# A new order of the mixing stage's stream, and new rules for when background steps are put in, in a two-layer fp32 decoder trunk

## The chip, the core and the metric

One core of a Trainium2 chip runs the whole program. The metric is device time in microseconds of one execution; the time of a kernel is the median of its runs. TensorE (PE) does the matmuls, VectorE (DVE) and ScalarE (ACT) the elementwise work, GpSimd (POOL) a few adds and small transfers, SyncE (SP) issues the weight loads. Each engine works through its own instructions in the order in which they were written, and waits where an input isn't there.

## What is computed

Two layers, each a half-step SwiGLU FFN, a mixing stage, and a second half-step FFN, over 256 tokens of width 1024, then a final RMS norm. The mixing stage is the part that changes:

```python
h = rms_norm(x, mix_norm[l])
(u, q_b, c_kv, q_i, k_i, w_i, q_c, k_c, v_c, f_c, g_a, g_b, g_c) = split(h @ w_in[l])
a = s5_branch(u, ...)                      # diagonal state space, then a GLU (w_glu)
b = dsa_branch(q_b, c_kv, q_i, k_i, w_i, ...)   # indexer picks 64 keys a query, then attention
c = fox_branch(q_c, k_c, v_c, f_c + fox_b_f[l]) # attention with a cumulative forget gate
merged = (sigmoid(g_a) * (a @ w_branch_ssm[l]) + sigmoid(g_b) * (b @ w_branch_dsa[l])
          + sigmoid(g_c) * (c @ w_branch_fox[l]))
x = x + merged @ w_out[l]
```

## The kernel before

**The stream.** Every weight matrix is cut into units of 2 x 128 rows and at most 512 columns (512 KB), in the order in which PE uses them (`plan`, whose mixing part follows the table `ORDER`). A unit is loaded by SP into one of four `raw` buffers, split by ACT into a rounded high part (`hi`) and by DVE into the rest (`lo<-raw,hi`), and multiplied on PE in three passes, hi x hi, lo x hi and hi x lo, for each of two halves of the tokens: 12 matmuls of 512 columns a unit. These matmuls write `ps_acc` and are called the stream here. The stream has nothing to wait for but its units, and its left side: `h0`, `h1` are the two halves of the normed input (h and l: high and low part), `ath`, `atl` the FFN's activations, `ahl` the state space's result, `bh`, `bl` the result of one of the two attentions.

**The background.** All else is written as Python generators that are stepped between the stream's matmuls while the program is built: `ssm` (state space; its matmuls read `u4` and `state`), `indexer` (scores and eight rounds of top-8 on DVE, then attention of DSA), `latent` (keys and values of DSA), `forget` (cumulative sums, sent through DRAM to the tiles `fm`), `fox` (attention of FoX), and the transposes of the next stage's input (`norm_T`, tiles `ps_t<-ident,...`). An attention (`attend`) goes in three pairs of heads. Each pair takes scores on PE (`kdT,qbT` or `kcT,qcT`), a sum with a bias and a minimum on DVE (`st,mn<-ps_t,bm` or `fm`; the biases come from POOL), four exponentials on ACT, a scaling by the sums' reciprocal, then for each head three transposes on PE (`ident,st`) and a copy to `pt`, and the product with the values (`pt,vd` or `pt,vs`), whose result is split into `bh` and `bl`. These matmuls write `ps_t`, in four banks that are used in turn.

**What sets the order.** `tick` is called after every three to six stream matmuls. It keeps a clock of its own for each engine, first splits ahead (`feed`: high parts up to 4 units ahead, low parts up to 3), and then steps the first background generator, by rank, whose input is ready by that clock and while neither DVE nor ACT is more than `BACKLOG` (1.25 us of that clock) ahead of PE. `rank` is 2 for the indexer and its attention, 1 for `latent` and `forget`, 3 for FoX, 4 for the state space, which counts as rank 0 from a set time on (`due`, in steps of `PACE`, 25 us). Where the stream comes to a branch whose attention isn't finished, `finish` steps that generator to its end with no stream in between.

**The table.** `ORDER` sets the mixing stage's second half. Before: both gates of DSA, both of FoX, one of the state space, branch DSA (first half of the output columns), branch FoX, gate SSM, GLU, then the other branches, SSM last. `merged` of a half is complete with its third branch; its transposes make the left side of `w_out`. The four gates of DSA and FoX and the first of the state space are 5 x 48 stream matmuls; all the rest of the second half, up to `w_out`, is 48 of gate, 24 short ones of the GLU and 96 of branches.

Of the kernel before, what the change touches and what calls it, by code (L numbers as in the profile page):

```python
# [41 lines left out]
SB, CH, NB = 4, 32, T // 4  # L42


ORDER = [("gate", "dsa", 0), ("gate", "dsa", 1), ("gate", "fox", 0), ("gate", "fox", 1), ("gate", "ssm", 0),
         ("branch", "dsa", 0), ("branch", "fox", 0), ("gate", "ssm", 1),
         ("glu", "ssm", 0), ("branch", "dsa", 1), ("branch", "ssm", 0), ("branch", "fox", 1), ("branch", "ssm", 1)]
GATE = {"ssm": 0, "dsa": 1, "fox": 2}
BRANCH_K = {"ssm": 2, "dsa": 3, "fox": 3}

# [5 lines left out]
HI_AHEAD, LO_AHEAD = 4, 3  # L56
# [4 lines left out]
LATENCY, SAME = 0.2, 0.13  # L61


TICK, BACKLOG, PREP, EAGER = 1.5, 1.25, 0.0, -0.5

FEED, PACE = 0.3, 25.0

LAST = 8

# [55 lines left out]
class Clock:  # L125
# [9 lines left out]
    def ready(self, ap, eng=None):  # L135
        t, by = self.done.get(ap.tensor.name, (0.0, eng))
        return t + (SAME if by == eng else LATENCY)
# [16 lines left out]
    def late(self, eng, cost, out, src):  # L154
        self.t[eng] += 1.0
        self.done[out.tensor.name] = max(self.t[eng], self.ready(src)) + cost + 3.0, "dma"
# [76 lines left out]
class Trunk:  # L233
    def __init__(self, ctx, tc, a, out):
        self.clock = Clock()
        self.tc, self.nc, self.a, self.out = tc, Engines(tc.nc, self.clock), a, out
        self.ctx = ctx
        nc = self.nc
        pool = lambda **kw: ctx.enter_context(tc.tile_pool(**kw))

        self.const = pool(name="const", bufs=1, side="right")
        self.rawp = pool(name="raw", bufs=RAW_BUFS, side="right")
        self.small = pool(name="small", bufs=2, side="right")
        self.hpool = pool(name="h", bufs=1, side="left")
        self.piecep = pool(name="piece", bufs=1, side="left")
        self.accp = pool(name="acc", bufs=4, space=PSUM)
        self.tp = pool(name="tps", bufs=T_BANKS, space=PSUM)
        self.dram = pool(name="scratch", bufs=2, space=DRAM)
        self.tlive, self.tcount = {}, 0
        self.bg, self.wait, self.rank, self.due, self.backlog = [], {}, {}, {}, {}  # L250

        self.units = plan(a)
        self.raw, self.split_tiles, self.freed = {}, {}, {}
        self.n_dma = self.n_hi = self.n_lo = self.n_used = 0
# [26 lines left out]
    def spawn(self, gen, rank=0, backlog=BACKLOG):  # L281
        self.rank[gen] = rank
        self.wait[gen] = None
        self.due[gen], self.backlog[gen] = math.inf, backlog
        self.bg.append(gen)
        return gen

    def urgency(self, g):
        return self.rank[g] if self.clock.t["pe"] < self.due[g] else 0

    def step(self, g):
        self.now = g
# [12 lines left out]
        w = self.wait[g]  # L305
        return self.clock.ready(w) if isinstance(w, bass.AP) else 0.0

    def feed(self):

        now, ready = self.clock.t["pe"] + FEED, self.clock.ready  # L310
        while self.n_hi < min(self.n_used + HI_AHEAD, self.n_dma) and ready(self.raw[self.n_hi]) <= now:
            self.feed_hi(self.n_hi + 1)
        while self.n_lo < min(self.n_used + LO_AHEAD, self.n_hi) and ready(self.split_tiles[self.n_lo]) <= now:
            self.feed_lo(self.n_lo + 1)

    def tick(self):
        t = self.clock.t
        now = t["pe"]
        while t["pe"] < now + TICK:
            self.feed()  # L320
            for g in sorted(self.bg, key=self.urgency):
                if not self.blocked(g) and self.when(g) <= t["pe"] + EAGER and max(t["dve"], t["act"]) <= now + self.backlog[g]:
                    self.step(g)
                    break
            else:
                return

    def finish(self, *gens):
# [351 lines left out]
    def mix(self, l, nxt):  # L680
# [5 lines left out]
        with tc.tile_pool(name="mix", bufs=1, side="left") as pool:  # L686
# [35 lines left out]

            self.rows_read = self.qk_read = False
            gen_x = self.spawn(self.indexer(l, xs), 2)
            gen_s = self.spawn(self.ssm(l, uT), 4)


            vs = pool.tile([P, 2, VW], F32, name="vs")
# [16 lines left out]
            for k0 in (0, 4):  # L745
                self.mm_col(pk, self.hx, k0, 4, 256, 0, 7)
            self.scaled(kcT[:, 1:3], pk, rb, 2)
            gen_f = self.spawn(self.fox(gen_g, qcT, kcT, vs), 3)

            qbT = pool.tile([P, 3, T], F32, name="qbT")  # L750
            pq = self.acc()
# [63 lines left out]
    def indexer(self, l, xs):  # L815
        nc, pool = self.nc, self.mp
        stt = nc.vector.scalar_tensor_tensor

        kd = pool.tile([P, 2, 2, HD], F32, tag="kd", name="kd")
        nc.vector.tensor_copy(kd, xs[:, :, KI:KI + HD].unsqueeze(2).to_broadcast([P, 2, 2, HD]))  # L820
        wi = pool.tile([P, 2, 4], F32, name="wi")
        self.ts(wi, xs[:, :, WI:WI + 4], 0.5)
        yield xs
        i, ps = yield from self.bank()
        for h in range(2):
            for t in range(2):
                nc.tensor.transpose(ps[:, h * T + t * P:h * T + t * P + P], xs[:, t, QI + h * P:QI + h * P + P], self.ident)
        yield ps
        qk = pool.tile([P, 3, T], F32, tag="bh2", name="qk")
        qiT, kiT = qk[:, :2], qk[:, 2]  # L830
        nc.scalar.activation(qiT, ps.rearrange("p (k t) -> p k t", k=2), AF.Copy, scale=0.125)
        self.tfree(i)
        yield kd
        i, ps = yield from self.bank()
        for t in range(2):
            nc.tensor.transpose(ps[:, t * P:t * P + P], kd[:, t].rearrange("p a b -> p (a b)"), self.ident)
        yield ps
        nc.scalar.activation(kiT, ps[:, :T], AF.Copy)
        self.tfree(i)
        yield kiT  # L840

        score = pool.tile([P, 384], F32, tag="pt1", name="score", bufs=2)
        for p in range(2):
            got = yield from self.banks()
            for q, k in ((slice(P, T), slice(0, T)), (slice(0, P), slice(0, P))):
                for e, (i, ps) in enumerate(got):
                    r = slice(e * HD, e * HD + HD)
                    o = ps[:, P:384] if q.start else ps[:, 0:P]
                    nc.tensor.matmul(o, qiT[r, p, q], kiT[r, k], start=True, stop=True)
            yield got[1][1]  # L850
            rel = pool.tile([P, 2, 384], F32, tag="st1", name="rel", bufs=2)
            for e, (i, ps) in enumerate(got):
                h = 2 * p + e
                nc.scalar.activation(rel[:, e], ps[:, :384], AF.Relu)
                self.tfree(i)
                for c, t, n in self.PARTS:
                    b = self.ccm[:, T - n:] if h == 0 else score[:, c]
                    stt(score[:, c], rel[:, e, c], wi[:, t, h:h + 1], b, op0=OP.mult, op1=OP.add)
                if e == 0:
                    yield  # L860
        self.qk_read = True

        sc = pool.tile([P, 2], F32, name="sc")
        for t in range(2):
            j = self.small.tile([P, 512], F32, tag="junk", name="junk", bufs=1)
            nc.scalar.activation(j[:, :P], xs[:, t, CKV:CKV + P], AF.Square, accum_out=sc[:, t:t + 1])
        latent = self.spawn(self.latent(l, xs, sc), 1)

        for rd in range(TOPK // 8):
            for c, t, n in self.PARTS:  # L870
                m8 = pool.tile([P, 8], F32, tag="m8", name="m8", bufs=2)
                nc.vector.max(m8, score[:, c])
                nc.vector.match_replace(score[:, c], m8, score[:, c], -3e38)
                yield
        madd = pool.tile([P, 384], F32, name="madd")
        self.ts(madd, score, -2e38, NEG, OP.is_gt, OP.mult)

        def bias(p):
            bm = pool.tile([P, 2, 384], F32, tag="bm", name="bm")
            for c, t, n in self.PARTS:  # L880
                nc.gpsimd.tensor_tensor(bm[:, :, c], madd[:, c].unsqueeze(1).to_broadcast([P, 2, n]),
                                        self.biasT[:, 2 * p:2 * p + 2, T - n:], op=OP.add)
            return bm

        yield latent
        yield lambda: self.rows_read
        yield from self.attend(self.qbT, lambda p, r: self.kdT[r, :], bias, lambda h, t: self.vd[:, t], "1")
# [162 lines left out]
    def ssm(self, l, uT):  # L1050
        nc, pool = self.nc, self.mp
        tt = nc.vector.tensor_tensor
        gen, begin = self.now, self.clock.t["pe"]
        quads = [(slice(m * CH, m * CH + CH), slice(i * CH, i * CH + CH), m, i) for m in range(4) for i in range(SB)]
        late = lambda n: self.due.__setitem__(gen, begin + n * PACE)
        late(0)
        yield uT

        u4 = pool.tile([P, 8, NB], F32, tag="u4", name="u4")
# [2 lines left out]
            if i == SB - 1:  # L1062
                yield

        late(1)
        w = pool.tile([P, 2, 8, NB], F32, tag="w", name="w")
        st = pool.tile([P, 2, 8, NB], F32, tag="st", name="state")
        half = [P, 2, 4, NB]
# [1 line left out]
        for h in (0, 4):  # L1070
# [31 lines left out]
            tt(st[:, 0, hs], g1[:, 0], g2[:, 1], op=OP.subtract)  # L1102
            tt(st[:, 1, hs], g1[:, 1], g2[:, 0], op=OP.add)
            yield
            late(2)

        late(3)
        yield st
        i, y = yield from self.bank()
        y = y.rearrange("p (c t) -> p c t", c=8)  # L1110
# [386 lines left out]
```

## Time and profile before

| | us |
|---|---|
| median of 3 runs (1246.01 to 1247.59) | 1246.51 |
| the profiled execution | 1247.36 |
| its span, first to last instruction | 1245.6 |
| PE busy in the span | 1189.1 (95%) |
| DVE busy | 789.2 (63%) |
| ACT busy | 605.2 (49%) |

The profile shows one execution. Its own time is 0.85 us above the median; sums over its rows are made against its own time. A matmul's end in the trace is modelled and overlaps the next one, so what a matmul costs is read from one start to the next. The two mixing stages lie at 210 to 437 us and at 822 to 1048 us.

### The profile page before, as it was taken

Reading aid. Unit: us, or ns where it says so; the run is one execution under the profiler, and the core shown is the slowest. Engines: PE = TensorE matmul, PEld = TensorE weight load, DVE = VectorE, ACT = ScalarE, POOL = GpSimd, SP = SyncE. Lnnn points to the kernel's source line nnn. Section 1 sums busy time; section 2 is a strip of 40 time slices with the busy share of each in tenths; the row PEclk is TensorE's granted clock in tenths of the full one; section 3 lists DMA queues with packets and bytes.
Section 4 is the critical chain, followed back from the end, with each engine's and each line's share of the span. In section 5 each row is a group of like instructions: output and inputs, shape, how many; then the busy total and the mean of one; then the engine's idle time right before and its main releaser. Section 6 shows DMA issues by size and latency. Waiting matters only on the chain. (4 is left out here: it accounts for less than half of the span.)

```text
span 1245.6 us, 16482 instructions
## 1 busy us (share of the span) xinstructions
PE 1189.1 (95%) x5990; PEld 992.7 (80%) x5990; DVE 789.2 (63%) x1382; ACT 605.2 (49%) x887; POOL 87.7 (7%) x135
## 2 busy tenths in 40 slices
PE   8999999999869899999999999999997789999997
PEld 6788888998648778888888888889885577888886
DVE  4886855787646665555577645567875575655554
ACT  5544444644544454444455445446546345544442
POOL 1000600000310510000000000000021000000000
PEclk9999999999879999999999999999999799999999
DMA  8665745575314566647565646555652155665552
GB/s 273 203 181 158 228 151 147 153 227 173 94 43 152 153 181 188 188 132 228 190 186 169 171 142 220 186 147 162 206 162 81 56 181 156 200 186 170 178 191 88
DMA packets 115554, 208.07 MB, mean 167 GB/s; under 512 B 7486, under 2 KB 27376, under 8 KB 115472
## 3 DMA queue, kind: packets, MB, share of 16 engines
q1 hardware_dynamic: 114000, 203.51, 53.8%
q0 software_dynamic: 1184, 3.11, 0.9%
q8 instruction: 47, 0.77, 0.3%
q10 hardware_dynamic: 288, 0.39, 0.1%
q14 instruction: 35, 0.29, 0.1%
HBM read 205.91 MB, written 1.07 MB: 166 GB/s over the span
## 5 line engine op out<-in xcount | busy, mean ns | idle before, releaser
L216 DVE TENSOR_TENSOR lo<-raw,hi 128x1024 fp32r<-128x1024 f32 (+3 forms) x415 | 472.1, 1143 | 291.1 <-PE ps_acc L216 208.6
L216 ACT ACTIVATE hi<-raw 128x1024 fp32r<-128x1024 f32 (+3 forms) x415 | 410.3, 991 | 459.5 <-PE ps_acc L216 397.9
L216 PE MATMUL ps_acc<-hi,h0h 128*128 128x512 f32 (+3 forms) x544 | 211.8, 389 | 7.2 <-ACT h0h L216 3.5
L216 PE MATMUL ps_acc<-hi,h0l 128*128 128x512 f32 (+3 forms) x544 | 206.1, 379 | 6.2 <-DVE h0l L216 6.2
L216 PE MATMUL ps_acc<-lo,h0h 128*128 128x512 f32 (+3 forms) x544 | 205.6, 378 | 2.0 <-DVE lo L216 2.0
L216 PE MATMUL ps_acc<-hi,h1h 128*128 128x512 f32 (+3 forms) x544 | 205.4, 377 | 0.0
L216 PE MATMUL ps_acc<-hi,h1l 128*128 128x512 f32 (+3 forms) x544 | 203.9, 375 | 0.0
L216 PE MATMUL ps_acc<-lo,h1h 128*128 128x512 f32 (+3 forms) x544 | 203.7, 375 | 0.0
L216 PE MATMUL ps_acc<-hi,ath 128*128 128x512 f32 x352 | 139.8, 397 | 0.0
L216 PE MATMUL ps_acc<-hi,atl 128*128 128x512 f32 x352 | 137.1, 390 | 0.0
L216 PE MATMUL ps_acc<-lo,ath 128*128 128x512 f32 x352 | 137.1, 389 | 0.0
L216 PEld LDWEIGHTS ps_acc<-hi,h0h 128*128 128x128 f32 x544 | 103.2, 190 | 26.9 <-ACT h0h L216 4.5
L216 PEld LDWEIGHTS ps_acc<-hi,h0l 128*128 128x128 f32 x544 | 103.0, 189 | 25.8 <-DVE h0l L216 7.5
L216 PEld LDWEIGHTS ps_acc<-lo,h0h 128*128 128x128 f32 x544 | 103.3, 190 | 19.7 <-DVE lo L216 3.5
L216 PEld LDWEIGHTS ps_acc<-hi,h1l 128*128 128x128 f32 x544 | 102.3, 188 | 17.9
L216 PEld LDWEIGHTS ps_acc<-hi,h1h 128*128 128x128 f32 x544 | 102.4, 188 | 17.8 <-issue 0.2
L216 PEld LDWEIGHTS ps_acc<-lo,h1h 128*128 128x128 f32 x544 | 102.5, 188 | 17.3
L216 PEld LDWEIGHTS ps_acc<-hi,ath 128*128 128x128 f32 x352 | 66.1, 188 | 14.1 <-issue 1.1
L216 PEld LDWEIGHTS ps_acc<-hi,atl 128*128 128x128 f32 x352 | 66.1, 188 | 14.1
L216 PEld LDWEIGHTS ps_acc<-lo,ath 128*128 128x128 f32 x352 | 66.1, 188 | 13.6 <-issue 0.5
L216 PE MATMUL ps_t<-ident,st 128*128 128x128 f32 x72 | 16.9, 371 | 29.6 <-ACT st L216 23.6
L216 DVE SCALAR_TENSOR_TENSOR act<-ps_acc,rstd,s 128x512 f32<-128x512 f32 (+1 forms) x48 | 32.0, 704 | 15.7 <-PE ps_acc L216 15.6
(270 smaller groups left out, 1266.7 us busy)
## 6 DMA issues: line engine op xcount, KB each, us to landing
raw<-in_ffn_w_down_dram SPq DMA_DIRECT2D x88, 512.0 KB, 4.2
raw<-in_ffn_w_up_dram SPq DMA_DIRECT2D x80, 512.0 KB, 3.8
raw<-in_ffn_w_gate_dram SPq DMA_DIRECT2D x79, 512.0 KB, 3.8
raw<-in_w_in_dram SPq DMA_DIRECT2D x56, 512.0 KB, 4.3
raw<-in_w_out_dram SPq DMA_DIRECT2D x16, 512.0 KB, 3.7
raw<-in_ffn_w_gate_dram SPq DMA_DIRECT2D x18, 256.0 KB, 2.8
raw<-in_ffn_w_up_dram SPq DMA_DIRECT2D x16, 256.0 KB, 2.8
raw<-in_w_in_dram SPq DMA_DIRECT2D x16, 256.0 KB, 2.8
```

The costliest lines, as they stand in the source:

```text
L216: return f(*args, **kw)
```

## The change

The table puts the state space first: its two gates, DSA's gates, the GLU, one gate of FoX, both branches of the state space, branch DSA, the last gate of FoX, and then the last three attention branches. The state space's rank becomes 3 and FoX's 4, `latent` goes from 1 to 2, and the due times are gone. In `tick`, low parts are first split only 2 units ahead and high parts 3; then background steps are taken, as long as DVE and ACT are within 8 us of PE (1.25 before) and the next low and high part still have room before the time at which PE will want them; only when no step is to be had are the parts split up to 3 and 4 ahead, as before. A step may be taken when its input is ready 0.2 us ahead of PE, 0.5 before. What is computed stays the same: PE has the same 5502 instructions in both programs.

```diff
-ORDER = [("gate", "dsa", 0), ("gate", "dsa", 1), ("gate", "fox", 0), ("gate", "fox", 1), ("gate", "ssm", 0),
-         ("branch", "dsa", 0), ("branch", "fox", 0), ("gate", "ssm", 1),
-         ("glu", "ssm", 0), ("branch", "dsa", 1), ("branch", "ssm", 0), ("branch", "fox", 1), ("branch", "ssm", 1)]
+ORDER = [("gate", "ssm", 0), ("gate", "ssm", 1), ("gate", "dsa", 0), ("gate", "dsa", 1), ("glu", "ssm", 0), ("gate", "fox", 0),
+         ("branch", "ssm", 0), ("branch", "ssm", 1), ("branch", "dsa", 0), ("gate", "fox", 1),
+         ("branch", "fox", 0), ("branch", "dsa", 1), ("branch", "fox", 1)]
...
-TICK, BACKLOG, PREP, EAGER = 1.5, 1.25, 0.0, -0.5
-
-FEED, PACE = 0.3, 25.0
+TICK, BACKLOG, PREP, EAGER = 1.5, 8.0, 0.0, -0.2
+
+
+FEED, FIRST, UNIT, LO_ROOM, HI_ROOM = 0.3, (3, 2), 2.7, 2.0, 3.5
...
+    def spare(self, i):
+
+        return self.clock.t["pe"] + sum(UNIT * m * n / 1024 for _, m, n in self.units[self.n_used:i])
+
+    def room(self, backlog, now):
+
+        dve, act = self.clock.t["dve"], self.clock.t["act"]
+        if max(dve, act) > now + backlog:
+            return False
+        return self.n_lo == len(self.units) or dve < self.spare(self.n_lo) - LO_ROOM and act < self.spare(self.n_hi) - HI_ROOM
...
         while t["pe"] < now + TICK:
-            self.feed()
-            for g in sorted(self.bg, key=self.urgency):
-                if not self.blocked(g) and self.when(g) <= t["pe"] + EAGER and max(t["dve"], t["act"]) <= now + self.backlog[g]:
+
+            self.feed(*FIRST)
+            for g in sorted(self.bg, key=self.rank.get):
+                if not self.blocked(g) and self.when(g) <= t["pe"] + EAGER and self.room(self.backlog[g], now):
                     self.step(g)
                     break
             else:
+                self.feed()
                 return
```

**First place: PE, DSA's attention in layer 0.** `ident,st` are the transposes of the weights of one head, `kdT,qbT` the scores of a pair, `pt,vd` and `pt,vs` the products with the values of DSA and FoX. Before, after the last matmul of the last gate:

```order
L216 MATMUL ps_acc<-hi,h1l 128x512
L216 MATMUL ps_t<-ident,st 128x128 x3
L216 MATMUL ps_t<-kdT,qbT 128x256 x2
L216 MATMUL ps_t<-kdT,qbT 128x128 x2
L216 MATMUL ps_t<-ident,st 128x128 x3
L216 MATMUL ps_t<-pt,vd 64x256 x2
L216 MATMUL ps_t<-pt,vd 64x128 x2
L216 MATMUL ps_t<-ident,st 128x128 x6
```

Now, at the last of DSA's first branch and the first of FoX's second gate:

```order
L217 MATMUL ps_acc<-lo,bh 128x512
L217 MATMUL ps_acc<-hi,bl 128x512
L217 MATMUL ps_t<-ident,st 128x128 x3
L217 MATMUL ps_acc<-hi,h0h 128x512
L217 MATMUL ps_acc<-lo,h0h 128x512
L217 MATMUL ps_acc<-hi,h0l 128x512
...
L217 MATMUL ps_t<-pt,vs 64x256 x2
L217 MATMUL ps_t<-pt,vs 64x128 x2
```

Before, steps of the attentions follow each other on PE; now stream matmuls stand between a head's transposes and the product that needs their copy, six of them here.

**Second place: PE, the end of the branches in layer 0.** `ident,gate` are the transposes of `merged`, `ahl` is the state space's branch, `h0h` after them the left side of `w_out`. Before:

```order
L216 MATMUL ps_acc<-lo,ahl 128x512
L216 MATMUL ps_acc<-hi,ahl 128x512
L216 MATMUL ps_t<-ident,gate 128x128 x8
L216 MATMUL ps_acc<-hi,h0h 128x512
L216 MATMUL ps_acc<-lo,h0h 128x512
L216 MATMUL ps_acc<-hi,h0l 128x512
L216 MATMUL ps_t<-ident,gate 128x128 x4
```

Now, in the last half unit of DSA's second branch, ahead of the 18 matmuls of FoX's second branch:

```order
L217 MATMUL ps_acc<-hi,bl 128x512
L217 MATMUL ps_t<-ident,gate 128x128 x4
L217 MATMUL ps_acc<-hi,bh 128x512
L217 MATMUL ps_acc<-lo,bh 128x512
L217 MATMUL ps_acc<-hi,bl 128x512
L217 MATMUL ps_t<-ident,gate 128x128 x4
```

Before, the first eight transposes stand right ahead of the matmul that needs their result; now the branch stands between.

**Third place: DVE, DSA's attention in layer 0.** `lo<-raw,hi` is the low part of a unit. Before:

```order
L216 ISA st,mn<-ps_t,bm 128x256
L216 ISA mn 128x1
L216 TENSOR_TENSOR lo<-raw,hi 128x1024 x2
L216 COPY vT<-v 32x128 x5
L216 TENSOR_TENSOR lo<-raw,hi 128x512
L216 COPY vT<-v 32x128 x3
L216 RECIPROCAL ri<-rs 128x4
```

Now:

```order
L217 ISA st,mn<-ps_t,bm 128x256
L217 ISA mn 128x1
L217 TENSOR_TENSOR lo<-raw,hi 128x1024
L217 COPY vT<-v 32x128 x8
L217 TENSOR_TENSOR bl<-ps_t,bh 128x256
L217 RECIPROCAL ri<-rs 128x4
L217 TENSOR_SCALAR st<-st,ri 128x256
L217 TENSOR_TENSOR lo<-raw,hi 128x1024
```

The low parts have moved behind steps of the attentions and of the state space.

## Rows read from the trace of the kernel before

**Rows 1.** Page, part 2: busy tenths in 40 slices of the span.
```profile
PE   8999999999869899999999999999997789999997
DVE  4886855787646665555577645567875575655554
```
**Rows 2.** Windows: stretch, length, busy (count) of PE, PEld, DVE, ACT, POOL; clock, DMA.
```profile
209.97:329.96 119.99, 119.99 (x732) 108.27 (x730) 94.73 (x221) 67.40 (x108) 11.06 (x13) 1.00 0.58 172
329.96:375.59 45.63, 30.62 (x143) 19.54 (x141) 21.17 (x76) 19.38 (x61) 7.76 (x7) 0.71 0.12 40
375.59:462.31 86.72, 81.86 (x375) 67.27 (x375) 58.59 (x83) 42.80 (x57) 21.84 (x44) 0.98 0.53 164
942.01:984.76 42.75, 27.63 (x143) 17.73 (x141) 21.23 (x76) 19.26 (x61) 7.61 (x7) 0.83 0.13 42
984.76:1073.16 88.40, 83.53 (x375) 68.59 (x375) 58.15 (x83) 42.79 (x57) 0.56 (x1) 0.95 0.53 167
```
**Rows 3.** Windows round single groups; a window's count includes a neighbour or two.
```profile
462.31:468.71 6.40, 6.40 (x33) 5.29 (x32) 4.63 (x7) 3.10 (x4) 0.00 (x0) 1.00 0.67 180
245.71:251.47 5.76, 5.76 (x51) 5.76 (x50) 5.26 (x25) 1.34 (x4) 0.00 (x0) 1.00 0.35 104
313.33:314.18 0.85, 0.85 (x10) 0.69 (x9) 0.12 (x1) 0.60 (x1) 0.85 (x1) 1.00 0.04 12
958.34:959.53 1.19, 1.19 (x9) 0.69 (x9) 0.89 (x5) 0.61 (x3) 0.00 (x0) 1.00 0.00 0
...
334.33:335.52 1.19, 0.00 (x0) 0.00 (x0) 1.19 (x9) 0.86 (x4) 0.00 (x0) 0.90 0.00 0
```
**Rows 4.** Chain of waits, a piece of the last FFN: start, us, what.
```profile
763.39 32.68 PE ps_acc L216 x144
```
**Rows 5.** Timeline of PE, layer 0's attentions; in brackets idle before, and releaser.
```profile
337.22 1.95 PE L216 MATMUL ps_t<-ident,st 128*128 128x128 f32 x6 [3.68 <-ACT st L216]
339.11 2.25 PE L216 MATMUL ps_t<-pt,vd 128*64 128x256 f32 x8
...
342.44 0.82 PE L216 MATMUL ps_t<-kcT,qcT 64*128 64x256 f32 x8
345.64 1.54 PE L216 MATMUL ps_t<-ident,st 128*128 128x128 f32 x6 [2.38 <-ACT st L216]
...
349.16 0.50 PE L216 MATMUL ps_acc<-hi,bh 128*128 128x512 f32 x1
...
371.93 1.54 PE L216 MATMUL ps_t<-ident,st 128*128 128x128 f32 x6 [3.10 <-ACT st L216]
...
375.59 0.79 PE L216 MATMUL ps_acc<-hi,bh 128*128 128x512 f32 x1
```
**Rows 6.** Timeline of PE and DVE, start of w_out and of layer 0's second FFN.
```profile
407.82 1.03 PE L216 MATMUL ps_t<-ident,gate 128*128 128x128 f32 x8
412.92 0.50 PE L216 MATMUL ps_acc<-hi,h0l 128*128 128x512 f32 x1 [3.09 <-DVE h0l L216]
...
412.18 1.28 DVE L216 SCALAR_TENSOR_TENSOR h0l<-ps_t,h0h 128x512 fp32r<-128x512 f32 x2
...
439.44 0.50 PE L216 MATMUL ps_acc<-hi,h0h 128*128 128x512 f32 x1 [1.52 <-ACT h0h L216]
```
**Rows 7.** Timeline of POOL: a pair of bias adds, beside low parts and alone.
```profile
319.51 2.94 POOL L216 TENSOR_TENSOR bm<-madd,biasT 128x256 f32<-128x256 f32 x2 [2.31 <-DVE mn L216]
...
335.67 1.97 POOL L216 TENSOR_TENSOR bm<-madd,biasT 128x256 f32<-128x256 f32 x2 [13.22 <-DVE mn L216]
```
**Rows 8.** Waits over the whole span: us in total, times, longest us.
```profile
DVE lo L216 <- PE ps_acc L216: 208.6, 145, 4.1
```
**Rows 9.** DMA issues: KB each, median us from issue to landing.
```profile
raw<-in_w_in_dram SPq DMA_DIRECT2D x56, 512.0 KB, 4.3
...
fm<-cumd POOLq DMA_DIRECT2D x6, 256.0 KB, 4.0
cumd<-cum POOLq DMA_DIRECT2D x2, 6.0 KB, 3.3
```

More of the change, by code (lines that the diff above doesn't have):

```diff
@@ L249, in __init__ @@
         self.tlive, self.tcount = {}, 0
-        self.bg, self.wait, self.rank, self.due, self.backlog = [], {}, {}, {}, {}
+        self.bg, self.wait, self.rank, self.backlog = [], {}, {}, {}
         self.units = plan(a)
@@ L283, in spawn @@
         self.wait[gen] = None
-        self.due[gen], self.backlog[gen] = math.inf, backlog
+        self.backlog[gen] = backlog
         self.bg.append(gen)
         return gen
-    def urgency(self, g):
-        return self.rank[g] if self.clock.t["pe"] < self.due[g] else 0
     def step(self, g):
@@ L306, in when, with feed @@
         return self.clock.ready(w) if isinstance(w, bass.AP) else 0.0
-    def feed(self):
+    def feed(self, hi=HI_AHEAD, lo=LO_AHEAD):
         now, ready = self.clock.t["pe"] + FEED, self.clock.ready
-        while self.n_hi < min(self.n_used + HI_AHEAD, self.n_dma) and ready(self.raw[self.n_hi]) <= now:
+        while self.n_hi < min(self.n_used + hi, self.n_dma) and ready(self.raw[self.n_hi]) <= now:
             self.feed_hi(self.n_hi + 1)
-        while self.n_lo < min(self.n_used + LO_AHEAD, self.n_hi) and ready(self.split_tiles[self.n_lo]) <= now:
+        while self.n_lo < min(self.n_used + lo, self.n_hi) and ready(self.split_tiles[self.n_lo]) <= now:
             self.feed_lo(self.n_lo + 1)
+    def spare(self, i):
[5 more added lines that the diff above has]
+        return self.n_lo == len(self.units) or dve < self.spare(self.n_lo) - LO_ROOM and act < self.spare(self.n_hi) - HI_ROOM
     def tick(self):
@@ L724, in mix @@
             gen_x = self.spawn(self.indexer(l, xs), 2)
-            gen_s = self.spawn(self.ssm(l, uT), 4)
+            gen_s = self.spawn(self.ssm(l, uT), 3)
             vs = pool.tile([P, 2, VW], F32, name="vs")
@@ L747, in mix @@
             self.scaled(kcT[:, 1:3], pk, rb, 2)
-            gen_f = self.spawn(self.fox(gen_g, qcT, kcT, vs), 3)
+            gen_f = self.spawn(self.fox(gen_g, qcT, kcT, vs), 4)
             qbT = pool.tile([P, 3, T], F32, name="qbT")
@@ L866, in indexer @@
             nc.scalar.activation(j[:, :P], xs[:, t, CKV:CKV + P], AF.Square, accum_out=sc[:, t:t + 1])
-        latent = self.spawn(self.latent(l, xs, sc), 1)
+        latent = self.spawn(self.latent(l, xs, sc), 2)
         for rd in range(TOPK // 8):
@@ L1052, in ssm @@
         tt = nc.vector.tensor_tensor
-        gen, begin = self.now, self.clock.t["pe"]
         quads = [(slice(m * CH, m * CH + CH), slice(i * CH, i * CH + CH), m, i) for m in range(4) for i in range(SB)]
-        late = lambda n: self.due.__setitem__(gen, begin + n * PACE)
-        late(0)
         yield uT
@@ L1063, in ssm @@
                 yield
-        late(1)
         w = pool.tile([P, 2, 8, NB], F32, tag="w", name="w")
@@ L1104, in ssm @@
             yield
-            late(2)
-        late(3)
         yield st
```

## Prediction

> **What bounds the kernel now.** I read the page's slices first: PE is busy nine tenths or more nearly everywhere, but falls to 8, 6, 9 and 7, 7, 8, 9 tenths near the ends of the two mixing stages, where DVE has no more to do than elsewhere [rows 1]. So PE bounds the time, and what a change of order can win is the time in which PE stands or runs slowly. The windows show where that is. Layer 0's mixing runs for its first 119.99 us with PE busy throughout, at full granted clock, though fourteen groups of background matmuls stand in that stretch and DVE is busy 94.73 us of it, 79% [rows 2]. Then come 45.63 us in which PE is busy 30.62, at a mean granted clock of 0.71, and 86.72 us with 81.86 busy; layer 1 repeats this with 42.75 and 88.40 us [rows 2]. The timeline shows what those 45.63 us are: the transposes wait 3.68, 2.38, 3.10 us for ACT's share of the softmax, with nothing else on PE [rows 5]. This is `finish`, called by the first attention branch with both attentions still open.
>
> What PE's work there would cost with nothing to wait for, by start-to-start times at full clock: 144 stream matmuls in 32.68 us, 0.227 each [rows 4]; 48 of 256 columns in 5.76, 0.12 each; 24 stream matmuls and 8 transposes in 6.40, so 0.95 for the 8, 0.12 each; a pair's scores 0.85; a pair's product with the values 1.19 [rows 3]. The 45.63 us hold 142 of these (a window counts a neighbour more): 36 transposes 4.3, five pairs of scores 4.25, six products 7.1 and 18 stream matmuls 4.1, in all 19.8. **Lost: 25.8 us in layer 0, and 22.9 of the same 19.8 in layer 1** (42.75). The next stretch holds 374: 318 stream matmuls 72.2, 24 short ones 2.9, 32 transposes 3.8, in all 78.9. **Lost: 7.8 and 9.5 us.** Its two visible places are the start of w_out, 3.09 us behind eight transposes put right ahead of their use, and the second FFN's first matmul, 1.52 us [rows 6]; most of the rest is the lower clock, 0.98 and 0.95. In sum 66.0 us of the two mixing stages are loss.
>
> **The change part by part.** *The table.* No instruction comes or goes on PE. The state space's gates take the place of FoX's as cover for the indexer, at no cost, since both have 48 matmuls of the same kind. What counts is that the attentions' steps now stand among stream matmuls: from the first scores of DSA to the last product of FoX 192 of them (43.6 us) and 24 short ones (2.9). In the order I count 23 background groups there in each layer, with 0.7 to 2.7 us of stream ahead of most.
>
> Is that enough for the chains? FoX's took 33.2 us in the open, from 342.44 to 375.59, with the clock at half for much of it [rows 5]. Between the same two steps PE now has 129 stream matmuls (29.3), 24 short ones (2.9), ten groups of three transposes (3.6), three of scores (2.6) and five products (6.0): 44.4 us. DSA's took 35.8, from 313.33 to 349.16 [rows 3, 5]; between its first scores and last product stand 135 stream matmuls (30.6), 24 short ones (2.9), eight groups of transposes (2.9), six of scores (5.1) and four products (4.8), 46.3 us, and the state space's output besides. So each chain has some 11 us to spare where it had none, and **25.8 and 22.9 us come back, less what single groups still wait.**
>
> *What single groups wait.* No row shows these steps in this cover, so I bound it. From below: 0, as in the first 119.99 us, with groups of the same length behind 0.7 to 5 us of stream [rows 2]. It can't be less, since a group costs its own time. From above: in the open a group waits 2.4 to 3.7 us [rows 5]; with some 2 us of stream ahead of each on average (46.5 over 23), the groups could wait about 1 us each, 23 us a layer. The row nearest is the covered stretch: DVE's load decides, and with 174.5 us of DVE work a layer over the 219 that remain (94.73 + 21.17 + 58.59, over 252.3 less the 33) it is 80%, against 79% there. I take 3 us a layer for the smaller margin (0.2 for 0.5 us), and keep 0 to 12 in the forecast.
>
> *The end of the branches.* The transposes of `merged`'s first half now stand 18 matmuls, 4.1 us, ahead of w_out. After them come two copies on ACT and two on DVE, which took 1.28 us at 412.18 [rows 6]. So the 3.09 us go in both layers, and nothing is late next: the second half has 21 matmuls of cover. The second FFN's first transposes stand 15 matmuls ahead of their use, where they stood 3 and 0, so the 1.52 us go too. Where PE was busy throughout the clock was 1.00 [rows 2], so the 7.8 and 9.5 us come back whole.
>
> *Background ahead of low parts.* In front of one low part, that of the unit used right after DSA's first product, DVE now has two pairs' sums, 1.19 us each [rows 3], a dozen short steps and the part itself: 5 to 6 us, an estimate from those rows. PE has 4.5 us of work from the unit before to that one (eleven stream matmuls, a pair's scores, a product). Cost on PE: nothing, if DVE is ahead by more than the difference. DVE waited 145 times for PE with a low part, 208.6 us in all [rows 8], so it is ahead as a rule; that cover gone, such a unit would cost about 1 us. SP's loads follow the low parts, which free the buffers; a unit lands in 4.3 us [rows 9], and four buffers hold 10.9 us of stream (48 matmuls), so they stay hidden.
>
> *POOL.* Its six pairs of adds a layer now all run beside low parts. FoX's first bias needs the sums' write (3.3 us), the read back (4.0) and a pair of adds of about 2: 9.3 us behind DVE's scan [rows 9, 7]; PE has 11.9 us of work from that scan's input to FoX's first scores. DVE stands still if it is late, and the low part behind it is wanted 9.9 us of PE's work on (24 stream matmuls, 24 short ones, two groups of transposes, one of scores). I take 0.
>
> *A rule against this.* A pair of adds took 2.94 us beside low parts, 1.97 alone [rows 7]. The Trainium skill says why ("SBUF — State Buffer", section "SBUF: two separate sides"): a DVE operation with two SBUF inputs and a GpSimd operation lock the same pair of ports, and the later one blocks. The trace agrees. By that rule alone, with all twelve pairs of both layers blocked by 0.97 us and each block passed on to PE, 11.6 us would be lost again and the time would be 1199; by the rows DVE has 20% idle to take it, and I leave it out of the sum.
>
> The FFNs keep their order but for the transposes of the activations, which move three to six matmuls on PE with none of them waiting now: 0.
>
> **The sum.** 1247.36 of the profiled execution, less 66.0, plus 6 for the groups: 1187.4; 0.85 less by the median: **1187**.
>
> **The rivals.** *Groups wait half a microsecond each.* The cover is right but margins are thin: scores behind a bank that DVE has yet to empty, products behind a copy in a full ACT queue. 46 groups at 0.5 are 23 in place of 6: 1204; at the full microsecond above, 1227. For it: DVE may be 8 us behind now. Against: the covered stretch.
>
> *The clock stays low.* If many short stops hold the granted clock at 0.71 over the attentions, as in the open stretch [rows 2], their 63 us a layer (stream 46.5, scores 5.1, transposes 4.3, products 7.1) take 89, 26 more, and the time is 1239, 0.6% faster. A rule points that way: the Trainium skill ("TensorE: Matmul & The Clock Gate", section "A second HAM failure mode: psum-queue depth-cycling") has the clock swing where matmul groups stop briefly again and again. Against it: 1.00 in the covered stretch, with its groups.
>
> *Low parts come late: slower.* All 67 units of a mixing stage now have background ahead of their low parts. If half of the 134 came 1 us late, as the one above would without a lead, 67 us replace the 66 won: 1254. It decides from 0.5 us a unit on average. Against: 208.6 us of DVE waiting for PE.
>
> *The plan doesn't do what it says.* Half of the steps could still be left to `finish`. The order speaks against it: no two products follow without stream between but in one place a layer. Half the attentions' loss kept is 24 us: 1211.
>
> **How the numbers follow.** Forecast 1187, with 0 to 12 us of waits a layer 1180 to 1204: 0.74. Groups wait longer, or half the plan, 1204 to 1227: 0.16. Clock, about 1239: 0.04. Late low parts, 1254: 0.06. The range leaves out the clock, the low parts and the upper half of the second case, and at the bottom a little for losses outside mixing that shift: 1178 to 1212. What a measurement can tell from no change is about 0.2%, 2.5 us. The clock's and the low parts' cases spread by some us, so 0.01 of each falls within it: faster 0.74 + 0.16 + 0.03, 0.93; same 0.02; slower 0.05.
>
> **What would show it.** Right: PE at 9 in the slices of both mixing stages; granted clock 1.00 there; mixing shorter by 30 us or more a layer; waits of `ps_t` for `st` down from several us to tenths. The thin-margin rival: waits of a few tenths at most groups. The low parts': `ps_acc` waiting for `lo`. The clock's: PE busy, clock under 0.9. Wrong from the start would be a stretch with products back to back and PE idle.

## The result, and the profile after

The changed kernel takes **1179.45 us** in the median (1179.25 to 1180.49), against 1247.05 for the kernel before on the same chip: a ratio of 0.9459, 95% interval 0.9443 to 0.9476. The profiled execution took 1179.28 us with a span of 1177.5, 68.1 less than before. The profile counts 5990 records on PE, as it did before.

Parts 1 and 2 of the page of after answer to [rows 1]: busy time of the engines, then PE and its granted clock in 40 slices.

```profile
PE 1164.3 (99%) x5990; PEld 979.4 (83%) x5990; DVE 781.5 (66%) x1370; ACT 607.1 (52%) x899; POOL 86.0 (7%) x135
...
PE   8999999999999999999999999999999999999997
...
PEclk9999999999999999999999999999999999999999
```

The dents at both mixing stages are gone. The windows of after answer to [rows 2] (columns as there): the covered stretch, the attentions from DSA's first scores to FoX's last product, and what follows, for each layer.

```profile
208.03:296.33 88.30, 88.30 (x562) 80.85 (x560) 74.97 (x179) 48.37 (x76) 5.09 (x6) 1.00 0.59 176
296.33:366.14 69.81, 69.07 (x399) 54.59 (x398) 51.41 (x127) 46.58 (x108) 12.75 (x14) 1.00 0.45 136
366.14:428.05 61.91, 61.91 (x289) 51.11 (x288) 44.56 (x68) 34.67 (x48) 21.82 (x44) 1.00 0.61 187
785.64:873.90 88.26, 88.26 (x562) 80.85 (x560) 74.97 (x179) 48.31 (x76) 5.09 (x6) 1.00 0.60 175
873.90:943.80 69.90, 69.16 (x399) 54.61 (x398) 50.59 (x127) 46.90 (x108) 12.78 (x14) 1.00 0.44 136
943.80:1005.71 61.91, 61.91 (x289) 51.13 (x288) 44.43 (x68) 34.67 (x48) 0.56 (x1) 1.00 0.62 196
```

The attentions now lie in 69.81 us with 399 matmuls, at clock 1.00, and PE misses 0.74 us of them. What PE waits for in the whole span (us in total, times, longest):

```profile
PE ps_acc L217 <- ACT hi L217: 1.8, 2, 1.3
PE ps_t L217 <- DVE ones L217: 1.1, 1, 1.1
PE ps_t L217 <- DVE mn L217: 0.9, 2, 0.5
PE ps_acc L217 <- DVE lo L217: 0.8, 1, 0.8
PE ps_acc L217 <- DVE ahl L217: 0.5, 2, 0.3
```

**Where the 68.1 us come from.** I measure a mixing stage from its first stream matmul to the first transposes of the second FFN's activations. It went from 254.4 to 222.1 us in layer 0 and from 253.2 to 222.1 in layer 1: 32.3 and 31.1, in sum 63.4. The other 4.7 lie outside: 1.9 ahead of the first mixing stage, 2.1 between the two, 0.7 behind the second.

### The profile page after: what moved, and what is told of

The parts are those of the page before. It is cut to its first block, busy times and chain, and to the rows that moved or that the text cites. A ratio compares the mean times of both kernels' runs of the same rounds, so it can differ in the third digit from the quotient of the medians.

```text
span 1177.5 us, 16466 instructions
## 1 busy us (share of the span) xinstructions
PE 1164.3 (99%) x5990; PEld 979.4 (83%) x5990; DVE 781.5 (66%) x1370; ACT 607.1 (52%) x899; POOL 86.0 (7%) x135
## 4 chain that ended last, share of the span: by engine, by line
PE 96%; ACT 2%; DVE 1%; DMA 1%; issue 0%; SPq 0%; ACTq 0%; DVEq 0%
PE ps_acc L217 88%; PE ps_t L217 8%; DMA raw<-in_ffn_w_gate_dram 1%; ACT vT L217 1%; ACT hi L217 0%; ACT st L217 0%; DVE lo L217 0%; SPq L217 0%; DVE st L217 0%; ACT ahl L217 0%; DVE rsqt L217 0%; DVE bl L217 0%; DVE rstd L217 0%; ACT bh L217 0%; ACT junk L217 0%
## 5 line engine op out<-in xcount | busy, mean ns | idle before, releaser
L217 PE MATMUL ps_acc<-hi,h1h 128*128 128x512 f32 (+3 forms) x544 | 208.1, 383 | 0.0
L217 PEld LDWEIGHTS ps_acc<-hi,ath 128*128 128x128 f32 x352 | 66.1, 188 | 13.6 <-issue 0.6
L217 DVE TENSOR_TENSOR atl<-ps_t,ath 128x512 fp32r<-128x512 f32 x44 | 30.4, 691 | 32.2 <-ACT ath L217 32.2
L217 ACT ACTIVATE ath<-ps_t 128x512 fp32r<-128x512 f32 x44 | 26.0, 594 | 31.1 <-PE ps_t L217 31.1
```

The source lines that it names most:

```text
L217: return f(*args, **kw)
```

## The experiments

All times stand beside the kernel before on the same chip; kernels are compared by their ratios to it, and by their mixing stages, measured as above.

| kernel | us | ratio, 95% interval | layer 0 | layer 1 |
|---|---|---|---|---|
| before | | 1 | 254.4 | 253.2 |
| after | 1179.5 | 0.9459 (0.9443–0.9476) | 222.1 | 222.1 |
| t1 table alone | 1229.9 | 0.9868 (0.9840–0.9896) | 246.9 | 242.2 |
| t2 rules alone | 1198.9 | 0.9628 (0.9597–0.9659) | 232.4 | 231.7 |
| t3 backlog 1.25 | 1225.4 | 0.9825 (0.9806–0.9844) | 240.2 | 241.9 |
| t4 no room rule | 1211.4 | 0.9706 (0.9670–0.9743) | 235.6 | 241.4 |
| t5 parts first | 1193.1 | 0.9560 (0.9546–0.9574) | 227.7 | 227.9 |
| t9 inputs 0.5 us ahead | 1193.4 | 0.9560 (0.9545–0.9574) | 228.9 | 228.5 |
| t12 the same, but the state space | 1185.1 | 0.9510 (0.9496–0.9525) | 224.2 | 223.9 |
| t7 gate behind DSA's branch | 1195.2 | 0.9590 (0.9567–0.9613) | 230.4 | 229.3 |
| t8 DSA's branch first | 1192.2 | 0.9562 (0.9539–0.9586) | 228.5 | 228.4 |
| t10 DSA's branch behind the gate | 1183.6 | 0.9504 (0.9490–0.9518) | 224.7 | 224.8 |
| t6 adds doubled | 1183.9 | 0.9506 (0.9491–0.9520) | 223.7 | 223.7 |
| t11 longer state space | 1187.2 | 0.9527 (0.9511–0.9543) | 226.3 | 225.3 |

### Which half brings it: t1, t2

t1 is the kernel before with the new `ORDER` and nothing else. t2 is the kernel after with these lines of before:

```diff
-            gen_s = self.spawn(self.ssm(l, uT), 3)
+            gen_s = self.spawn(self.ssm(l, uT), 4)
...
-            gen_f = self.spawn(self.fox(gen_g, qcT, kcT, vs), 4)
+            gen_f = self.spawn(self.fox(gen_g, qcT, kcT, vs), 3)
...
-        latent = self.spawn(self.latent(l, xs, sc), 2)
+        latent = self.spawn(self.latent(l, xs, sc), 1)
```

and the old `ORDER`.

> Only the new table of foreground work, put into the kernel before; its planner's rules and ranks stay. Theory A (table and rules are both needed): with the old rules the background is let in too late to use the longer stretch of gates and branches, two pairs of each attention are left with no foreground work beside them in either layer, at the 44.4/4 = 11.1 us that a pair's chain took, so some 4 x 18 = 72 us is lost again and the time is 1235 to 1255, near the kernel before. Theory B (the table alone brings it, by giving the chains more work to lie beside): 1180 to 1200. The feed-forwards' 4.7 us are the rules' by both, so they should read as before.

> Only the new rules of the planner (backlog, room, order of the parts), with the old table and the old ranks. Theory A (both are needed): DSA is covered now, since its chain starts earlier, but FoX's last two pairs still stand alone ahead of its branch, at 11.1 us a pair less some 2 us of PE's own groups: about 18 us a layer, and the clock falls there; 1179 + 36 to 50 = 1215 to 1230. Theory B (the rules alone bring it): 1180 to 1190. Theory C (the table alone brings it): 1235 to 1247. The feed-forwards should read as in the changed kernel (some 4.7 us less than before).

Neither half depends on the other. In the mixing stages the table alone wins 7.5 and 11.0 us, the rules alone 22.0 and 21.5: 62.0 in sum, where both together win 63.4. So theory A falls, and so do the theories of one half alone; the rules bring about two thirds. The new ranks are in neither half, so they and any interplay share the 1.4 us that are left.

What t1 lacks is not only the attentions. One line of its waits shows the state space late, by 5.8 us a layer:

```profile
PE ps_acc L216 <- ACT ahl L216: 11.5, 2, 5.8
```

My price was wrong too. The 11.1 us are right for a pair of FoX in the open (33.2 over three; the 44.4/4 in the text is a slip), but that is the pair's whole length, and PE's own work in it costs the same anywhere. In the PE timeline of t2 this is what FoX's last two pairs wait:

```profile
349.33 0.87 PE L217 MATMUL ps_t<-ident,st 128*128 128x128 f32 x6 [2.64 <-ACT st L217]
350.51 1.88 PE L217 MATMUL ps_t<-pt,vs 128*64 128x256 f32 x8 [0.31 <-ACT pt L217]
353.91 1.54 PE L217 MATMUL ps_t<-ident,st 128*128 128x128 f32 x6 [1.51 <-ACT st L217]
```

t2 loses 10.3 and 9.6 us a layer against after; 1.06 of it is a stop at the start of `w_out`, and the rest is some 4.5 for each open pair, clock included. The 25.8 us that the prediction found for five pairs, 5.2 each, come near.

### The planner's rules one by one: t3, t4, t5, t9, t12

```diff
t3:
-TICK, BACKLOG, PREP, EAGER = 1.5, 8.0, 0.0, -0.2
+TICK, BACKLOG, PREP, EAGER = 1.5, 1.25, 0.0, -0.2
t4, in room():
-        return self.n_lo == len(self.units) or dve < self.spare(self.n_lo) - LO_ROOM and act < self.spare(self.n_hi) - HI_ROOM
+        return True
t5, in tick():
-            self.feed(*FIRST)
+            self.feed()
t9:
-TICK, BACKLOG, PREP, EAGER = 1.5, 8.0, 0.0, -0.2
+TICK, BACKLOG, PREP, EAGER = 1.5, 8.0, 0.0, -0.5
t12, in tick():
-self.when(g) <= t["pe"] + EAGER and
+self.when(g) <= t["pe"] + (EAGER if self.rank[g] == 3 else -0.5) and
```

> The changed kernel with the planner's backlog at its old 1.25 instead of 8.0: a background step goes in only where VectorE and ScalarE are nearly idle by the plan. Theory A (the backlog is what lets the chains keep up with the longer stretch): the eight state-space groups and FoX's last pair stand without foreground work beside them, 8 to 9 us for the pair and up to 5 us for the groups in a layer, with the clock's loss 1200 to 1215. Theory B (the order of parts and the room rule do it): 1179 to 1184.

The backlog matters more than theory A said, and in another place. PE's waits in t3:

```profile
PE ps_acc L217 <- ACT ahl L217: 15.0, 2, 7.5
PE ps_t L217 <- DVE gate L217: 5.4, 4, 1.8
PE ps_t L217 <- DVE state L217: 4.5, 2, 2.2
```

`ahl` is the split output of the state space; the matmul that waits is the first of the GLU. It is the state space that comes late, by 7.5 us a layer, not FoX. These 7.5, the 2.2 for `state`, the 2.7 for `gate` and the clock make 17 of the 18.2 us that layer 0 loses: the granted clock is 0.50 from 322.89 to 339.95 us, where PE works for 9.03 us, and half of that is lost.

> The changed kernel without the room rule: background steps go in whether or not the next low parts are due. The prediction's rival of late low parts says that PE then waits for them, at 0.5 us a unit over the units of the stretch (20 to 30 a layer): 10 to 15 us a layer, 1199 to 1209, shown as idle time of PE released by VectorE's lo. If the three units that are split ahead are buffer enough, 1178 to 1183.

Here is the rival of late low parts. With no room rule the steps go in early: FoX's last product stands at 348.03 us, not 365.34. They take VectorE over where the low parts need it. PE's waits in t4, and a window round DSA's first scores (278.86):

```profile
PE ps_acc L217 <- DVE lo L217: 9.4, 12, 1.6
PE ps_t L217 <- DVE qbT L217: 6.1, 2, 3.1
PE ps_t L217 <- DVE mn L217: 3.7, 2, 1.8
```

```profile
249.00:282.00 33.00, 25.52 (x179) 22.45 (x178) 32.24 (x97) 11.27 (x16) 1.94 (x2) 0.95 0.55 168
```

VectorE is busy 32.24 of 33.00 us while PE stands 7.5. The loss is 13.5 and 19.3 us a layer, of which the low parts' waits make 4.7; queries (`qbT`) and scores (`mn`) that wait for VectorE as well, 4.9 a layer, and the lower clock make the rest. The clock is also what sets the layers apart: it is 0.50 for 6.8 us in layer 0 (from 278.60 and from 305.92 us) and for 20.5 in layer 1 (from 869.12 and from 903.25). The median lies 2 us above the band expected, by less than the runs differ among themselves (1206.2 to 1216.4).

> The changed kernel with the old order of work: four high parts and three low parts are split ahead before any background step, not three and two. The parts take VectorE's time just where the softmax steps are wanted, one low part of 1.22 us ahead of a step. If that order matters, each of the 23 groups a layer comes up to 1.2 us later, which the 11 us of slack takes in part: 1181 to 1190. If the room rule and the backlog do it all: 1179, within 1.5.

> The changed kernel with a step let in only when its input is ready 0.5 us ahead of PE by the plan, as before, instead of 0.2. If the waits that are left (3.6 us a layer) come from groups that PE reaches a little early, some of them go and the chains get longer by 0.3 us a step: 1176 to 1179. If they come from elsewhere (a bank that VectorE holds) and the chains' slack is used up: 1179 to 1185.

They cost 5.7 and 6.6 us a layer, more than any of the theories allowed, and by the same wait. First t5's, then t9's line of PE's waits:

```profile
PE ps_acc L217 <- ACT ahl L217: 7.2, 2, 3.6
```

```profile
PE ps_acc L217 <- ACT ahl L217: 10.6, 2, 5.3
```

In after the GLU's matmuls wait 0.27 us for `ahl`: this chain ends as PE arrives. From this I formed the theory that the state space, not an attention, has no slack.

> The run with inputs ready 0.5 us ahead took 1193.4 us and PE waited 5.3 us for the state space's gating input in layer 0. Here every background chain but the state space's has 0.5, and the state space keeps 0.2. Theory (the loss is the state space's lateness): the wait goes and the time is 1177 to 1184. Rival (the attentions' chains have used up their slack with the later steps): 1189 to 1194 as in that run.

With the state space alone kept at 0.2 the wait falls to 0.7 us in its longest, and 4.7 of the 6.6 us a layer come back; the time is 1.1 us over the theory's band and well under the rival's. The state space's lateness is most of t9's loss. Of the other 2 us a layer, 1.4 show at the attentions: the last products of DSA and of FoX take 1.50 us each, from their start to the next matmul, where they take 0.75 and 0.80 in after.

### How much the chains have to spare: t7, t8, t10, t6, t11

The table's middle in after is: GLU, gate FoX 0, branches SSM 0 and 1, branch DSA 0, gate FoX 1.

```diff
t7: GLU, branches SSM 0 and 1, branch DSA 0, gate FoX 0, gate FoX 1
t8: GLU, branch DSA 0, branches SSM 0 and 1, gate FoX 0, gate FoX 1
t10: GLU, gate FoX 0, branch DSA 0, branches SSM 0 and 1, gate FoX 1
```

> The changed kernel with one gate of 10.9 us moved from ahead of DSA's first branch to behind it: DSA's chain has that much less work beside it. The working of the prediction (10.6 to 11 us spare) expects 0 to 3 us lost a layer, so 1179 to 1186. If the chains ended long before their branch (much more than 11 us spare), nothing is lost: 1179. If they had no room to spare, the whole 10.9 us a layer is lost and the clock with it: 1200 or more.

t7 doesn't measure what it was made for. PE's timeline where it stands:

```profile
332.08 0.79 PE L217 MATMUL ps_acc<-hi,ahl 128*128 128x512 f32 x1 [4.26 <-ACT ahl L217]
```

This is the state space's first branch, waiting for ScalarE and VectorE to make the GLU's output. The gate that I moved had covered that, and 4.26 of the 7.2 to 8.3 us lost a layer are this wait.

> The changed kernel with DSA's first branch ahead of the two state-space branches and the gate: 16.3 us less beside DSA's chain. By the prediction's slack of some 11 us the chain is 5 us too long in each layer, and one pair stands alone: 5 to 9 us a layer, 1189 to 1198, the clock falling for a moment behind it. If the slack is larger than 16 us: 1179 to 1181. If there is no slack: 16.3 us a layer, 1212.

```profile
327.52 0.86 PE L217 MATMUL ps_t<-pt,vd 128*64 128x256 f32 x6 [1.33 <-DVE pt L217]
331.59 1.24 PE L217 MATMUL ps_t<-ident,st 128*128 128x128 f32 x6 [3.21 <-ACT st L217]
```

One pair of DSA stands open, as expected, and 6.4 us a layer are lost, inside the band. By itself this agreed with 11 us of slack. The next run does not.

> The changed kernel with DSA's first branch ahead of the two state-space branches but still behind the gate: 5.4 us less beside DSA's chain, and the gate still stands between the state space's gating product and the branches, which it did not in the two runs that took cover away. With 11 us to spare on DSA's chain nothing is lost: 1179 to 1181. If that chain is the tight one: 5.4 us a layer and the clock, 1190 to 1193.

The 5.4 us taken away cost 2.6 a layer. Here DSA's last pair waits, in the PE timeline of t10:

```profile
340.58 0.30 PE L217 MATMUL ps_t<-ident,st 128*128 128x128 f32 x1 [0.94 <-DVE st L217]
341.04 0.44 PE L217 MATMUL ps_t<-ident,st 128*128 128x128 f32 x2 [0.16 <-ACT st L217]
341.41 1.58 PE L217 MATMUL ps_t<-pt,vd 128*64 128x256 f32 x8
```

So there is no reserve of 11 us: at both sizes tried, two fifths to a half of what is taken is lost (2.6 of 5.4, 6.4 of 16.3). Why not all of it is lost wasn't tested; FoX's rank lies behind DSA's, so its steps can give way. The timeline of after shows why there is little left:

```profile
348.23 0.87 PE L217 MATMUL ps_t<-pt,vs 128*64 128x256 f32 x8
348.93 0.82 PE L217 MATMUL ps_t<-pt,vd 128*64 128x256 f32 x8
349.68 0.50 PE L217 MATMUL ps_acc<-hi,bh 128*128 128x512 f32 x1
```

DSA's last product stands right ahead of its branch, and a product of FoX ahead of that: whatever cover is there, the planner has filled.

```diff
t6, the DSA bias:
-                nc.gpsimd.tensor_tensor(bm[:, :, c], madd[:, c].unsqueeze(1).to_broadcast([P, 2, n]),
+                for _ in range(2):
+                    nc.gpsimd.tensor_tensor(bm[:, :, c], madd[:, c].unsqueeze(1).to_broadcast([P, 2, n]),
t11, the end of ssm():
         self.geT = self.halves(vT, "w")
+        for _ in range(4):
+            nc.scalar.activation(self.geT[0], vT, AF.Copy, scale=0.5)
```

> The changed kernel with GpSimd's additions of DSA's bias done twice (2.3 us more for each of its three pairs, with the same result), everything else in its place. Theory of the prediction (DSA's chain has some 11 us to spare, the state space is the tight one): 7 us more on DSA's chain costs 0 to 2 us a layer, 1179 to 1184. Rival of the prediction (what GpSimd needs for a pair is passed on to PE): 2.3 us a pair, 13.6 us, 1193.

> The changed kernel with one ScalarE copy at the very end of the state space's chain done five times (4 x 0.55 = 2.2 us more, the same result). Theory (this chain ends just as PE reaches the gating product, it has no slack): PE waits 2 us longer there in each layer, 1183 to 1187, shown as an idle time released by ahl. If the state space has the attentions' 11 us to spare: 1179 to 1181.

t6: 6.3 us more of DSA's adds a layer (26.1 us in all, 13.6 in after) cost 1.6, so GpSimd's time is not passed on to PE one for one, and the rival's 1193 falls. The time lies in the band of 11 us to spare, but how much of the added time lies on DSA's chain wasn't shown, so this doesn't outweigh t10. Half of what is lost shows in one line of PE's waits that after doesn't have, the forget gate's transposes:

```profile
PE ps_t L217 <- DVE ft L217: 1.5, 2, 0.8
```

t11: 2.2 us more on the state space's chain cost 4.2 and 3.2. PE's timeline of t11 at the GLU, and the window behind it:

```profile
326.05 0.79 PE L217 MATMUL ps_acc<-ahl,hi 128*128 128x256 f32 x2 [3.04 <-ACT ahl L217]
```

```profile
326.05:346.00 19.95, 19.95 (x100) 16.68 (x101) 10.58 (x28) 12.83 (x32) 4.78 (x5) 0.86 0.42 130
```

The wait grew from 0.27 to 3.04 us, by all that was added (the four copies take 0.66 us each, not the 0.55 expected), and then PE runs at a mean clock of 0.86 for 20 us. The time, 1187.2, is at the upper end of the theory's band. The state space has no slack: shown. None of the variants beats the kernel after.

## Why the prediction was right, and where its steps were not

The forecast was 1187, the time 1179.45, 0.6% lower. Its sum was 66.0 us won in mixing less 6 of new waits, 60, and 0 elsewhere; measured are 63.4 and 4.7.

**The loss was mis-sized by one row.** A pair's product was priced at 1.19 us from [rows 3], six a layer. That row holds a short wait of its own: the second head's matmuls start 0.40 us behind the first's (958.73 and 958.34), as VectorE's copy to `pt` ends at 958.68; in after they start 0.01 apart. Two products of after, in windows from their start to the next matmul:

```profile
314.05:314.85 0.80, 0.80 (x9) 0.49 (x8) 0.80 (x1) 0.80 (x5) 0.55 (x1) 1.00 0.19 72
348.93:349.68 0.75, 0.75 (x12) 0.44 (x8) 0.68 (x2) 0.55 (x3) 0.00 (x0) 1.00 0.89 289
```

At 0.80, twelve products cost 4.7 us less, and the loss to be won back was 70.7, not 66.0.

**What single groups wait** was taken at 3 us a layer, between 0 and 12. Of 70.7, 63.4 came back, so it is 3.6. The one visible place a layer is FoX's second pair of scores, in after's PE timeline:

```profile
323.82 0.70 PE L217 MATMUL ps_t<-kcT,qcT 64*128 64x256 f32 x2
324.98 0.92 PE L217 MATMUL ps_t<-kcT,qcT 64*128 64x256 f32 x6 [0.47 <-DVE mn L217]
```

The group takes 2.01 us from its start to the next matmul (325.83) where others take 0.85: VectorE, with a low part and a scaling ahead of its reductions, has not yet emptied the bank. That is the place which the rival of half a microsecond named ("scores behind a bank that DVE has yet to empty"), once a layer and not at 23 groups. With the wait at `ahl`, which holds the second GLU matmul back by 0.5 us (0.63 from the first one's start, where 0.12 would do), this is 1.7 us; the other 2.0, found by subtraction only, are 0.1 for each of 23 groups.

**"Each chain has some 11 us to spare" was the wrong step.** The conclusion held, since every product is in time, but PE's work between a chain's first and last step in the new order is no measure of slack when a planner sets that order: t10 loses 2.6 of 5.4 us. And the chain that is tight got no price at all, only the words "and the state space's output besides". t1, t3, t5, t9 and t11 all lose time there. In after it comes 0.27 us late; 0.3 us more on its steps make t9's wait of 5.3, and by t12 4.7 of t9's 6.6 us a layer. The prediction didn't see this margin: that the forecast held there was luck.

**The end of the branches and the second FFN** went as worked out, the 3.09 and 1.52 us of [rows 6] are gone in both layers. In after's PE timeline neither the transposes nor the first matmul of `w_out` has an idle time before it:

```profile
376.00 0.60 PE L217 MATMUL ps_t<-ident,gate 128*128 128x128 f32 x4
...
381.74 0.39 PE L217 MATMUL ps_acc<-hi,h0h 128*128 128x512 f32 x1
```

**The clock** came back whole, 1.00 in all six windows above, and that rival (1239) falls. The Trainium skill's "TensorE: Matmul & The Clock Gate", section "A second HAM failure mode: psum-queue depth-cycling", would have it swing where groups stop briefly again and again. This trace hardly puts that to the test: PE's visible stops in a layer's attentions are one of 0.27 and one of 0.47 us. Falls after single stops of 1.8 us and more are in t4, t9 and t11 (below).

**Low parts.** Right in after: one wait of 0.8 us in the whole span. But the reason given, that VectorE waits for PE for 208.6 us [rows 8], was not the one that counts. In t4 the same rival comes true and costs 13.5 to 19.3 us a layer. What holds it off is the room rule, which the prediction described and gave no price.

**POOL at 0** held for PE, but its premise was wrong: the pairs of adds do not all run beside low parts. GpSimd's adds of both attentions, after and then before (busy, mean ns, idle before):

```profile
L217 POOL TENSOR_TENSOR bm<-madd,biasT 128x256 f32<-128x256 f32 (+1 forms) x12 | 13.6, 1158 | 172.0 <-DVE madd L217 124.5 <-DVE mn L217 45.2 <-DVE ft L217 2.3
L217 POOL TENSOR_TENSOR fm<-fm,ccm 128x256 f32<-128x256 f32 (+1 forms) x12 | 12.2, 1019 | 9.6 <-DMA fm<-cumd 9.1
```

```profile
L216 POOL TENSOR_TENSOR fm<-fm,ccm 128x256 f32<-128x256 f32 (+1 forms) x12 | 14.1, 1173 | 1.2 <-DMA fm<-cumd 0.7
L216 POOL TENSOR_TENSOR bm<-madd,biasT 128x256 f32<-128x256 f32 (+1 forms) x12 | 13.7, 1166 | 44.1 <-DVE mn L216 31.1 <-DVE madd L216 13.0
```

They take 25.8 us in all, against 27.8. In after only the first of the six pairs of a layer meets a low part. From the DVE and POOL timelines of after:

```profile
273.08 1.22 DVE L217 TENSOR_TENSOR lo<-raw,hi 128x1024 fp32r<-128x1024 f32 x1
273.25 2.90 POOL L217 TENSOR_TENSOR bm<-madd,biasT 128x256 f32<-128x256 f32 x2 [62.18 <-DVE madd L217]
```

Its first add takes 1.64 us, in the other five pairs 0.72 to 0.77. Before, two pairs a layer were held up so by a low part (layer 0: at 319.51 and 353.13), which is the 2.0 us between the sums. The adds hold VectorE up as well: a scaling of 256 columns beside one takes 1.39 us in after, alone 0.35. So where an add meets a low part, the trace agrees, by 0.9 us, with the rule of the Trainium skill ("SBUF — State Buffer", section "SBUF: two separate sides") that the later of the two is blocked. What fails is the case built on it, twelve blocked pairs and 1199: ten of the twelve meet no low part, and PE has no stop after the other two.

**The FFNs** were taken at 0. Between the two mixing stages 2.1 us went, before and then after:

```profile
464.36:822.01 357.65, 356.50 (x1736) 298.51 (x1735) 205.20 (x247) 169.26 (x211) 0.00 (x0) 1.00 0.60 180
```

```profile
430.10:785.64 355.54, 355.54 (x1736) 298.57 (x1735) 204.68 (x247) 170.23 (x211) 0.00 (x0) 1.00 0.60 181
```

PE stood 1.15 us there before and no longer does. The prediction said that the transposes of the activations move "with none of them waiting now"; one group waited 1.03 us at 762.45 of before, and no row of the prediction covers that place. All runs with the new rules have 355.5 to 355.7 here. But t1, with the old rules, has 356.07, with the same order of instructions on PE, VectorE and ScalarE in this stretch as before: 1.6 of the 2.1 us went there without the change, so they can't be put down to it. The 1.9 us ahead of the first mixing stage are no surer (up to 3.5 of the 68.1 us may then not be the change's): in t6, t7, t8 and t10, whose rules are the same up to there, it begins anywhere from 206.2 to 208.9 us, and at 208.03 in after.

## What to carry to other kernels

Where a planner fills PE's idle time, ask of every chain how late it may end, the smallest one first: here a chain that took no part in the loss before, the state space's, has no room left, and 0.3 us more on each of its steps cost 4.7 us of the mixing stage in each layer (t9 against t12). A rule that lets more background in needs its counterpart that keeps the foreground's own parts in time; one without the other lost 32 us (no room rule) and 46 (the old backlog) of the 68. Price an operation by a row that waits for nothing, and check it against a second row of the same operation.

## What the runs showed of the hardware

One stop of PE can be enough to halve its clock for a while. In t4's timeline, in a stretch that is otherwise full from 278.86 us on, PE stops for 1.83 us; the stream matmuls behind it follow each other by 0.43 us, and from 309.38 on by 0.23 again. The window of that piece has a granted clock of 0.50, 1.2 GHz in place of 2.4:

```profile
305.00 0.92 PE L217 MATMUL ps_t<-kcT,qcT 64*128 64x256 f32 x6 [1.83 <-DVE mn L217]
...
306.41 0.63 PE L217 MATMUL ps_acc<-lo,h0h 128*128 128x512 f32 x1
306.84 0.63 PE L217 MATMUL ps_acc<-hi,h0l 128*128 128x512 f32 x1
...
309.38 0.39 PE L217 MATMUL ps_acc<-hi,h0l 128*128 128x512 f32 x1
309.61 0.39 PE L217 MATMUL ps_acc<-hi,h0h 128*128 128x512 f32 x1
```

```profile
306.00:309.30 3.30, 3.30 (x8) 2.62 (x9) 1.11 (x7) 2.40 (x8) 2.74 (x3) 0.50 0.65 210
```

Not every such stop does it. t1 stops for 2.53 us at the start of `w_out` in both layers: in layer 0 the granted clock falls to 0.50 behind it (407.70 to 411.00 us), in layer 1 it stays at 1.00 (1006.20 to 1016.00). What decides between the two isn't shown.

After t9's stop of 5.30 us the mean clock of the next 14.4 us is 0.83. So a wait can cost more than itself: t11's grew by 2.8 us and its mixing stages by 4.2 and 3.2. The stops of 0.47 us in after and of 0.94 in t10 brought no fall.
